# Weight sums started in the first half, stored blocks reloaded later, one activation sum moved by a product, held weights loaded into other buffers

## The chip, the cores and the metric

The kernel runs on one core of a Trainium2 chip. The metric is the device time of one execution in microseconds (us), the median over the runs shown. Five engines work side by side and meet only at semaphores: PE (matrix products), DVE (elementwise work on vectors), ACT (activation functions and copies), POOL (a second elementwise engine) and SP, which here issues every DMA transfer, one after the other in a fixed order.

## The reference

One decoder layer over 1024 tokens of 1024 features, in float32:

```
h   = rms_norm(x)
mix = [rwkv7_head_group(h), conformer_conv_group(h)] @ w_out
x   = x + rms_norm(mix)
h   = rms_norm(x)
hid = causal_conv3(h @ ffn_up)            # 1024 -> 2 * 2816 columns, 3 taps along the tokens
f   = (gelu(hid[:, :2816]) * hid[:, 2816:]) @ ffn_down
x   = x + rms_norm(f)
```

The change is only in the last part: the up projection, the gate and the down projection of the feed-forward block.

## The kernel before

**Precision.** Each float32 operand of a matmul is split into a rounded part and the rest, `hi` and `lo`. A product is then three matmuls: hi by hi, hi by lo and lo by hi. `split` (L154) lets ACT copy the rounded part and another engine subtract it to get the rest: POOL for streamed weights, DVE for activations. `weight` (L159) takes a buffer of tag `wr` (three of them, 128x512 floats each), lets SP load 256 KB into it, and splits it to `wh` and `wl` (two buffers each). With `held=True` the two parts go to buffers of the pool `h` instead, which stay full until the last product, and DVE rather than POOL makes the rest.

**Up projection.** Tokens are taken in two halves of 512. The 2816 gated columns are 22 blocks of 128. `ffn_pair` (L861 on) makes one gated block of one half: two projections of 1024 by 128 by 512, each with two weight tiles, then bias, three-tap convolution, gelu and product. Of the first half, blocks 0 to 11 are computed inside the mixer stage, wherever PE has room. Blocks 0 to 7 stay in on-chip rows; blocks 8 to 11 are stored to memory (`early`) and loaded back by `ffn_up` (L887 on; the load is L901). `ffn_up` then makes the ten blocks left of the first half, and after it the 22 of the second half. After some of these pairs it advances a generator `side` by one step, in a context that puts the step's DVE and POOL instructions behind the pair's last gate product and last weight split on these engines. DMA issues, ACT and PE instructions of the step are not bound by it.

The generator of the first half is the norm of the second half's rows (`norm_ffn`, L820 on): four steps, one for each 128 rows, and then `channels`, which transposes the last rows and writes their hi and lo parts. `islice` stops after four, so `channels` stands in the program behind all ten pairs. The generator of the second half is `weight_sums` (L915 on): 11 steps, each of which loads four 256 KB blocks of `ffn_down` into buffers of tag `tp` (eight of them), makes four sums on POOL (L918) and stores them to memory (L924 to L930). It is advanced after every second pair.

**Down projection.** `ffn_down` (L948 on) computes the product of the 1024 by 2816 gated matrix with the 2816 by 1024 weights as a 2 by 2 block scheme with seven block products in place of eight, called P1 to P7 here in the order of the code. Each has 11 steps `j`; a step splits one activation block (`a`, eight pairs of buffers ahead), splits one weight tile, and issues 12 matmuls. P1, P3, P5 and P7 sum into the four banks X, and P2, P4 and P6 into the four banks Y. P1, P3 and P7 take blocks of `ffn_down`, the others take the stored sums. Between them DVE makes the activation sums: in P4 `A22 += A21`, in P5 `A11 = A22 - A11` and then `A12 = A12 - A11`. P6 reads A11 and P7 reads A12. Seven weight tiles of P7 are held: `hold` loads and splits them during P5 (four) and P6 (three), so that P7 can end bank by bank. `second` after P6 and `last` after P7 finish the rows: norm, residual row from memory (`x1d`, L940), store to `out` (L946).

**Buffers of tag `f2`.** Six of 128x512 floats, used one after another by the up projection's accumulators, the norm's pieces, P2's activation differences, the scratch of P3's norm, and the residual rows of `ffn_out`.

**Order.** A planner orders each engine's instructions before the run, by priority (the place in the program, moved ahead for blocks marked high priority) and by its own estimate of times. Whatever has its inputs and its buffer may be placed ahead of work that stands earlier in the program. Buffers of one tag are given out in that order. On the chip each engine, and SP's queue of transfers, keeps the planned order: an instruction that waits holds all those behind it.

Of the kernel before, what the change touches and what calls it, by code (L numbers as in the profile page):

```python
# [4 lines left out]

# [8 lines left out]
F32 = mybir.dt.float32  # L14
# [38 lines left out]
EARLY, KEPT, EVERY = 12, 8, 2  # L53
# [42 lines left out]
class Trunk:  # L96
# [62 lines left out]
    def weight(self, src, shape, home=None, held=False):  # L159

        with self.tc.high_priority():
            raw = self.wp.tile(shape, F32, tag="wr", bufs=3, name=self.nm("wr"))
            self.nc.sync.dma_start(raw, src)
            if held:
                hi, lo = (self.hp.tile(shape, F32R, tag="h", name=self.nm("w")) for _ in range(2))
            elif home:
                hi, lo = (home[0].tile(shape, F32R, tag=t, bufs=BUFS[t], name=self.nm("wm")) for t in home[1:])
            else:
                hi, lo = (self.wp.tile(shape, F32R, tag=t, bufs=2, name=self.nm(t)) for t in ("wh", "wl"))
            self.low = self.split(hi, lo, raw, not held)[1]  # L170
        return hi, lo
# [715 lines left out]
    def ffn_up(self, h, hs, side, every, early=()):  # L887

        temp = lambda: self.f2p.tile([P, HALF], F32, tag="f2", name=self.nm("acc"))
        acts = []  # L890
        for i in range(FT):
            if i < min(KEPT, len(early)):
                acts.append(early[i])
                continue
            if h == 1 and i < 2 * KT:
                act = self.hp.tile([P, HALF], F32, tag="h", name=self.nm("act"))
            else:
                act = self.ap.tile([P, HALF], F32, tag="act", name=self.nm("act"))
            acts.append(act)
            if i < len(early):  # L900
                self.nc.sync.dma_start(act, early[i])  # L901
                continue
            self.ffn_pair(h, hs, i, temp, act)
            if (i - len(early)) % every == every - 1:
                with self.tc.issue_after(self.gated.ins), self.tc.issue_after(self.low.ins):
                    next(side, None)
        return acts
# [40 lines left out]
    def ffn_down(self, acts):  # L948
        nc = self.nc
        first = self.tc.high_priority  # L950
        A11, A12, A21, A22 = acts[0][:HT], acts[0][HT:], acts[1][:HT], acts[1][HT:]
        B = lambda r, c: lambda j: self.a["ffn_down"][c, r * HT + j]
        T = lambda n: lambda j: self.sums[n - 1, j]
        X = [self.bank() for _ in range(4)]
        Y = [self.bank(("pb", "pn")[t // 2]) for t in range(4)]
# [3 lines left out]
        def tt(out, a, b, op=ALU.add):  # L959
            nc.vector.tensor_tensor(out, a, b, op)  # L960
            return out
# [4 lines left out]
        def product(banks, src, wt, start, after, then=lambda j: None, held=(), soon=True):  # L966
            ops, n = [], HT - len(held)
            for j in range(HT):
                with first():
                    hi, lo = self.pair("a", self.h1p)  # L970
                    self.split(hi, lo, src(j))
                    then(j)
                wh, wl = self.weight(wt(j), [P, 512]) if j < n else held[j - n]
                op = (hi, wh), (hi, wl), (lo, wh)
                if j >= n:
                    ops.append(op)
                else:
                    for t in range(4):
                        mms(banks[t], t, op, start and j == 0, j == HT - 1)

            ins = []
            for t in range(4):
                for i, op in enumerate(ops):
                    ins += mms(banks[t], t, op, False, i == len(held) - 1)
                with first() if soon else ExitStack():
                    after(t)
            self.chain(ins)
# [27 lines left out]
        def after5(j):  # L1015
            hold(j, 3)
            tt(A11[j], A22[j], A11[j], ALU.subtract)
            tt(A12[j], A12[j], A11[j], ALU.subtract)

        product(Y, lambda j: A22[j], T(4), False, lambda t: tt(c21[t], s1[t], Y[t]), after4)  # L1020
# [12 lines left out]
            norm(0, t, 1, s1[t], s1[t], X[t])  # L1033
            self.ffn_out(t, (c11[t], s1[t]))

        product(Y, lambda j: A11[j], T(2), True, second, hold, soon=False)
        product(X, lambda j: A12[j], B(1, 1), False, last, held=late)


    def run(self):  # L1040
        self.setup()
        sts = [{}, {}]
        with ExitStack() as ctx:
            self.setup_mixer(ctx)
            h0, early = self.mixer(sts)
        with ExitStack() as ctx:
            self.setup_ffn(ctx)
            h1 = []
            norm = self.norm_ffn(1, lambda: self.row("nrow", 4),
                                 lambda: self.f2p.tile([P, HALF], F32, tag="f2", name=self.nm("m")), h1, 3,  # L1050
                                 pool=self.h1p)
            acts = [self.ffn_up(0, h0, islice(norm, 4), 1, early)]
            list(norm)
            side = self.weight_sums()
            acts.append(self.ffn_up(1, h1, side, EVERY))
            list(side)
            self.ffn_down(acts)

    def mixer(self, sts):
# [227 lines left out]
```

## Time and profile before

| | us |
|---|---|
| median of 3 runs | 1325.73 (1325.17 to 1326.6) |
| the profiled execution | 1324.09 |
| its span | 1322.3 |
| PE busy in the span | 1266.0 (96%) |
| DVE, ACT, POOL busy | 879.0, 680.5, 614.1 |
| up projection of the first half's last ten blocks starts, by the first of its matmuls | 727.4 |
| first matmul of the tile `w` (the held weights of P7) | 1292.5 |

PE is the engine to watch: it is busy nearly all of the time, and wherever it is idle the end moves. A view by stages gives, for each stretch of the span, the busy time of each engine (with the number of instructions), the granted PE clock as a share of full speed, the busy share of the DMA engines and the rate in GB/s. A row of a timeline gives start, duration, engine, line, operation, output from inputs and, in brackets, how long the engine had been idle and what released it. A row of waits gives who waited for whom: total us, times, longest.

### The profile page before, as it was taken

What the parts mean: (1) busy time and instruction counts of PE and PEld (TensorE: products, weight loads), DVE (VectorE), ACT (ScalarE), POOL (GpSimd) and SP (SyncE); (2) the same over time, 40 slices, a digit from 0 to 9 for tenths busy, and PEclk for the clock granted to TensorE, in tenths of its full rate; (3) what the DMA queues carried; (4) which work ended last, traced back from release to release, by engine and by line L of the source; (5) the groups of instructions that cost most, each with busy time, mean ns of one, the idle gap of its engine ahead of it and who ended that gap; (6) DMA issues with size and microseconds to landing.
All of it is one profiled execution on the core that took longest, in us unless ns stands there. A gap on an engine that the chain in (4) does not pass through costs nothing.

```text
span 1322.3 us, 22962 instructions
## 1 busy us (share of the span) xinstructions
PE 1266.0 (96%) x8580; PEld 1018.6 (77%) x8580; DVE 879.0 (66%) x1450; ACT 680.5 (51%) x1354; POOL 614.1 (46%) x522
## 2 busy tenths in 40 slices
PE   6999989999899989999999999999999999999996
PEld 5767767787679867787799778888888887877785
DVE  5376998997699979895521454355555559279447
ACT  6563654657655764656643464433433344543451
POOL 4343423344333422444463444476766666454541
PEclk9999989999999988999999999999999999999999
DMA  6222211121123441222354843356565643333436
GB/s 216 80 78 62 65 49 49 50 73 49 56 69 105 128 170 34 73 65 79 91 154 137 296 158 91 95 175 205 170 209 170 206 134 115 96 113 115 133 95 206
DMA packets 85647, 155.79 MB, mean 118 GB/s; under 512 B 9280, under 2 KB 15808, under 8 KB 85536
## 3 DMA queue, kind: packets, MB, share of 16 engines
q1 hardware_dynamic: 85536, 154.33, 38.0%
q8 instruction: 67, 1.10, 0.4%
q14 instruction: 44, 0.36, 0.1%
HBM read 129.13 MB, written 25.17 MB: 117 GB/s over the span
## 4 chain that ended last, share of the span: by engine, by line
PE 70%; DVE 14%; ACT 4%; issue 4%; DMA 4%; POOL 3%; SPq 0%; POOLq 0%; ACTq 0%; DVEq 0%
PE pb L130 57%; PE pe L130 4%; DVE pc L399 4%; PE xs L130 3%; POOL wl L157 2%; PE pn L130 2%; DVE dw L576 1%; DMA wr<-sums 1%; ACT wh L157 1%; DVE nrow L960 1%; PE pe L145 1%; DMA b<-ffn_down 1%; DVE kk L469 1%; DVE h L263 1%; DVE pt L468 1%
## 5 line engine op out<-in xcount | busy, mean ns | idle before, releaser
L157 POOL TENSOR_TENSOR wl<-wr,wh 128x512 fp32r<-128x512 f32 x350 | 468.0, 1338 | 536.7 <-ACT wh L157 509.0
L130 PE MATMUL pb<-f,wh 128*128 128x512 f32 x1408 | 444.2, 397 | 2.8 <-ACT pb L771 1.8
L157 ACT CAST wh<-wr 128x512 fp32r<-128x512 f32 x350 | 215.0, 615 | 325.0 <-PE pb L130 169.7
L130 PEld LDWEIGHTS pb<-f,wh 128*128 128x128 f32 x1408 | 264.4, 189 | 62.4 <-ACT pb L771 2.0
L130 PE MATMUL pb<-f,wl 128*128 128x512 f32 x704 | 281.0, 399 | 3.0 <-POOL wl L157 2.8
L130 PE MATMUL pb<-h,wh 128*128 128x512 f32 (+3 forms) x720 | 228.9, 398 | 2.0 <-ACT wh L157 1.4
L877 DVE SCALAR_TENSOR_TENSOR acc<-pb,params,acc 128x511 f32<-128x511 f32 (+1 forms) x128 | 95.5, 746 | 174.1 <-ACT acc L872 116.6
L399 DVE SCALAR_TENSOR_TENSOR pc<-c,params,pc 128x512 f32<-128x512 f32 x232 | 174.2, 751 | 4.6 <-ACT pc L396 0.5
L130 PEld LDWEIGHTS pb<-f,wl 128*128 128x128 f32 x704 | 133.0, 189 | 38.1 <-POOL wl L157 7.2
L130 PEld LDWEIGHTS pb<-h,wh 128*128 128x128 f32 (+2 forms) x720 | 131.5, 188 | 34.1 <-ACT wh L157 3.3
L130 PE MATMUL pb<-h,wl 128*128 128x512 f32 (+3 forms) x360 | 146.2, 406 | 2.8 <-POOL wl L157 2.6
L130 PE MATMUL pb<-wh,a 128*128 128x512 f32 x428 | 140.2, 395 | 1.5 <-ACT wh L157 1.5
L130 PEld LDWEIGHTS pb<-wh,a 128*128 128x128 f32 x428 | 80.3, 188 | 21.1 <-ACT wh L157 1.9
L130 PE MATMUL pb<-wl,a 128*128 128x512 f32 x214 | 85.3, 398 | 1.7 <-POOL wl L157 1.5
L130 PEld LDWEIGHTS pb<-h,wl 128*128 128x128 f32 (+2 forms) x360 | 67.5, 188 | 21.9 <-POOL wl L157 5.4
L157 DVE TENSOR_TENSOR a<-act,a 128x512 fp32r<-128x512 f32 x50 | 41.5, 837 | 41.8 <-ACT a L157 41.8
L157 ACT CAST a<-act 128x512 fp32r<-128x512 f32 x50 | 31.1, 621 | 63.5 <-PE pn L130 40.1
L877 DVE SCALAR_TENSOR_TENSOR pt<-pb,params,pt 128x511 f32<-128x511 f32 (+1 forms) x48 | 35.8, 746 | 35.7 <-ACT ecarry L874 35.3
L918 POOL TENSOR_TENSOR b<-b,b 128x512 f32<-128x512 f32 x44 | 58.3, 1324 | 0.9
L130 PEld LDWEIGHTS pb<-wl,a 128*128 128x128 f32 x214 | 40.2, 188 | 13.3 <-POOL wl L157 3.8
L872 ACT ACTIVATE acc<-pb,params 128x512 f32<-128x512 f32 x64 | 49.5, 773 | 1.8 <-PE pb L130 1.8
L130 PE MATMUL pn<-wh,a 128*128 128x512 f32 x132 | 46.7, 394 | 0.0
(297 smaller groups left out, 1947.1 us busy)
## 6 DMA issues: line engine op xcount, KB each, us to landing
wr<-ffn_up SPq DMA_DIRECT2D x176, 256.0 KB, 2.7
wr<-w_in SPq DMA_DIRECT2D x80, 256.0 KB, 2.6
b<-ffn_down SPq DMA_DIRECT2D x44, 256.0 KB, 3.9
sums<-b SPq DMA_DIRECT2D x44, 256.0 KB, 2.9
wr<-sums SPq DMA_DIRECT2D x44, 256.0 KB, 2.7
wr<-ffn_down SPq DMA_DIRECT2D x33, 256.0 KB, 2.6
wr<-w_out SPq DMA_DIRECT2D x32, 256.0 KB, 2.7
mixd<-t SPq DMA_DIRECT2D x16, 256.0 KB, 3.7
```

Source lines behind the costliest of these rows:

```text
L130: return self.nc.tensor.matmul(out, lhsT, rhs, start=start, stop=stop, skip_group_check=skip)
L145: self.nc.tensor.transpose(out, in_, self.con("ident")[:n, :n])
L157: return self.nc.scalar.copy(hi, src), eng.tensor_tensor(lo, src, hi.bitcast(F32), ALU.subtract)
L263: self.mark_lo = nc.vector.scalar_tensor_tensor(lo[:, toks], pv, g, hi[:, toks].bitcast(F32), ALU.mult, ALU.subtract)
L399: nc.vector.scalar_tensor_tensor(out, c[:, j:j + HALF], w(j), acc, ALU.mult, ALU.add)
L468: nc.vector.tensor_tensor_scan(sg[:, l], self.con("scan"), sg[:, l], 0.0, ALU.mult, ALU.add)
L469: nc.vector.scalar_tensor_tensor(kk[:, l], k[:, l], self.par("k_k", 2 * pp + l), kk[:, l], ALU.mult, ALU.mult)
L576: nc.vector.tensor_tensor(dv[:, j + 1:, :j], dv[:, j + 1:, :j], tv, ALU.add)
L872: nc.scalar.activation(acc, ps, AF.Identity, scale=w(2), bias=self.par("fb", ch))
L877: nc.vector.scalar_tensor_tensor(acc[:, o:], ps[:, :HALF - o], w(j), acc[:, o:], ALU.mult, ALU.add)
L918: sub = lambda o, x, y, op=ALU.subtract: nc.gpsimd.tensor_tensor(o, x, y, op)
L960: nc.vector.tensor_tensor(out, a, b, op)
```

## The change

Four edits, all in the feed-forward part.

1. The first half's `side` is now one generator that first runs the whole norm, `channels` included, and from its fifth step on advances `weight_sums` at every second step. With ten pairs these are steps 5, 7 and 9, so three of the eleven sum steps fall into the first half. The second half goes on with the other eight, still one after every second pair.
2. The four stored blocks are loaded back by DMAs that stand in the program behind the first half's ten pairs. Their buffers are taken at the same place as before.
3. `A12 = A12 - A11` moves from P5's hook to P6's.
4. The raw copy of a held weight is loaded into a buffer of tag `f2` instead of `wr`.

```diff
     def weight(self, src, shape, home=None, held=False):
 
         with self.tc.high_priority():
-            raw = self.wp.tile(shape, F32, tag="wr", bufs=3, name=self.nm("wr"))
+            raw = (self.f2p.tile(shape, F32, tag="f2", name=self.nm("wr")) if held else
+                   self.wp.tile(shape, F32, tag="wr", bufs=3, name=self.nm("wr")))
             self.nc.sync.dma_start(raw, src)
...
             if i < len(early):
-                self.nc.sync.dma_start(act, early[i])
                 continue
...
         def after5(j):
             hold(j, 3)
             tt(A11[j], A22[j], A11[j], ALU.subtract)
+
+        def after6(j):
+            hold(j)
             tt(A12[j], A12[j], A11[j], ALU.subtract)
...
-        product(Y, lambda j: A11[j], T(2), True, second, hold, soon=False)
+        product(Y, lambda j: A11[j], T(2), True, second, after6, soon=False)
         product(X, lambda j: A12[j], B(1, 1), False, last, held=late)
...
-            acts = [self.ffn_up(0, h0, islice(norm, 4), 1, early)]
-            list(norm)
-            side = self.weight_sums()
-            acts.append(self.ffn_up(1, h1, side, EVERY))
-            list(side)
+            sums = self.weight_sums()
+
+            def side():
+                yield from norm
+                while True:
+                    next(sums, None)
+                    yield
+                    yield
+
+            acts = [self.ffn_up(0, h0, side(), 1, early)]
+            for act, e in zip(acts[0][KEPT:], early[KEPT:]):
+                self.nc.sync.dma_start(act, e)
+            acts.append(self.ffn_up(1, h1, sums, EVERY))
+            list(sums)
             self.ffn_down(acts)
```

More of the change, by code (lines that the diff above doesn't have):

```diff
@@ L2 @@
 from contextlib import ExitStack, contextmanager
-from itertools import islice
 from types import SimpleNamespace
```

## The prediction

> **What bounds the kernel.** First the page's head and its busy line, then the stages of the feed-forward part.
>
> ```profile
> span 1322.3 us, 22962 instructions
> ...
> PE 1266.0 (96%) x8580; PEld 1018.6 (77%) x8580; DVE 879.0 (66%) x1450; ACT 680.5 (51%) x1354; POOL 614.1 (46%) x522
> ```
>
> ```profile
> 720.00:740.00 20.00, 18.20 (x102) 15.83 (x102) 3.35 (x5) 5.84 (x16) 3.86 (x3) 1.00 0.59 209
> 740.00:760.00 20.00, 18.41 (x77) 13.55 (x77) 12.66 (x18) 10.41 (x22) 9.66 (x9) 1.00 0.80 287
> 760.00:780.00 20.00, 19.48 (x88) 15.47 (x87) 10.84 (x16) 12.38 (x27) 9.99 (x10) 1.00 0.52 170
> 780.00:840.00 60.00, 60.00 (x278) 49.73 (x277) 25.73 (x43) 30.40 (x66) 28.05 (x23) 1.00 0.35 106
> 860.00:1080.00 220.00, 220.00 (x941) 176.72 (x940) 114.28 (x175) 86.60 (x137) 152.23 (x119) 1.00 0.58 184
> 1080.00:1100.00 20.00, 19.18 (x80) 14.54 (x80) 14.87 (x16) 12.05 (x21) 15.73 (x11) 1.00 0.41 132
> 1186.00:1217.00 31.00, 30.87 (x133) 24.53 (x132) 30.90 (x35) 14.04 (x28) 16.48 (x11) 1.00 0.45 144
> 1217.00:1250.00 33.00, 30.79 (x131) 24.22 (x130) 17.33 (x26) 14.79 (x26) 15.04 (x12) 1.00 0.40 121
> 1250.00:1281.00 31.00, 31.00 (x134) 24.92 (x134) 11.42 (x19) 13.60 (x24) 15.43 (x12) 1.00 0.41 118
> ```
>
> The first number behind each comma is PE's busy time. The last four stretches follow the products: P7 ends with PE at 1312.3 (row below), a product has 132 matmuls, and 220 us for 941 make 0.234 us each, so 31 us; P7 runs from 1281, P6 from 1250, P5 from 1217 with a gap in it, P4 from 1186. PE is the bound, at full clock (1.00). The change adds and removes no matmul, so it can only win PE's gaps or open new ones. They are few: 1.80, 1.59 and 0.52 us at the start, 0.82 at 1080, 0.13 at 1186 and 2.21 at 1217. From 780 to 840 and from 860 to 1080 there is none. PE's own waits from 640 on say what ended them:
>
> ```profile
> PE pb L130 <- POOL wl L157: 3.7, 9, 0.7
> PE pb L130 <- ACT pb L771: 1.8, 1, 1.8
> PE pb L130 <- ACT wh L157: 1.5, 1, 1.5
> ```
>
> The 1.8 behind L771 is the end of the mixer's output projection, which no edit touches. All else, 1.59 + 0.52 + 0.82 + 0.13 + 2.21 = 5.27 us, is PE waiting for a split weight tile. That is the whole prize: 0.4% of the run.
>
> **Held weights by other buffers, and the moved sum (edits 4 and 3).** The largest gap, in a timeline of SP, ACT, DVE and POOL where P4 ends and P5 begins, with the row of SP's waits that goes with it:
>
> ```profile
> 1211.52 0.33 SPq L163 DMA_DIRECT2D wr<-ffn_down  x1
> 1214.42 7.16 SPq L163 DMA_DIRECT2D wr<-sums  x3
> 1221.67 0.38 SPq L163 DMA_DIRECT2D wr<-ffn_down  x1
> ...
> 1214.16 0.62 ACT L157 CAST w<-wr 128x512 fp32r<-128x512 f32 x1 [1.67 <-DMA wr<-ffn_down]
> ...
> 1214.87 5.29 DVE L157 TENSOR_TENSOR a<-act,a 128x512 fp32r<-128x512 f32 x5
> 1220.08 0.68 DVE L157 TENSOR_TENSOR w<-wr,w 128x512 fp32r<-128x512 f32 x1
> ...
> 1224.28 1.82 POOL L157 TENSOR_TENSOR wl<-wr,wh 128x512 fp32r<-128x512 f32 x1 [4.67 <-ACT wh L157]
> ...
> SPq L163 <- DVE w L157: 11.2, 7, 6.0
> ```
>
> The first held tile is loaded at 1211.5 into one of three `wr` buffers. ACT has rounded it at 1214.8, but DVE makes its rest only at 1220.1, behind five activation splits. Until 1220.8 a third of the stream's buffers is gone and SP stands before its next transfer (the wait of 6.0). The weight tile behind it is split at 1224.3, and PE has lost 2.21 us. SP waited so for each of the seven held tiles, 11.2 us in all; by the windows only the long wait reached PE. So cover is about 6.0 - 2.2 = 3.8 us, an estimate: a shorter wait at SP is free.
>
> Edit 4 takes the held tiles out of `wr`, and the stream has its three buffers throughout. That removes this wait at its root, whatever DVE does: 2.2 us. The bounds are 1.5 (the ACT wait alone) and 2.2. The seven loads of 256 KB stay, in other places: six `f2` buffers are free when P3's scratch is done, and the place shows in what SP fills them with now:
>
> ```profile
> 1185.91 3.46 SPq L940 DMA_DIRECT2D x<-x1d  x6
> ```
>
> Six residual rows, needed only after P6. Held loads stand earlier in the program, so they should take these six places, at the same size and time. The 0.13 us lost from 1186 to 1217 therefore stays. The residual rows come one by one as held tiles are split; they are wanted by `second` after 1281, at least 30 us later, and cost nothing unless SP has to wait for their buffers (a rival below).
>
> Edit 3 moves eleven sums on DVE:
>
> ```profile
> L960 DVE TENSOR_TENSOR act<-act,row 128x512 f32<-128x512 f32 x8 | 8.5, 1069 | 0.0
> ...
> L960 DVE TENSOR_TENSOR act<-act,row x8: 677/688/1784, 1170.0 to 1204.4; 128x512 f32<-128x512 f32 x8
> ```
>
> Eleven at 1.07 us are 11.8 us. DVE is busy for 30.90 of 31 us in P4, where these sums of P5's hook are executed ahead of time, and for 11.42 of 31 in P6: moved there, P6 has 23.2 of 31 and PE still does not wait. P7's first splits need A12 and come up to eight blocks ahead, some 22 us, which is the cover. The planner may place part of them into the same early gaps as now, since A11 is ready; then DVE's load stays and only its order is better. Either way I count 0 on PE beyond edit 4: at most it shares the same 2.2 us.
>
> **Weight sums three steps earlier (edit 1).** The last step of `weight_sums` at present meets P1's first tiles on POOL:
>
> ```profile
> 1088.11 3.06 POOL L918 TENSOR_TENSOR b<-b,b 128x512 f32<-128x512 f32 x2
> 1091.14 1.81 POOL L157 TENSOR_TENSOR wl<-wr,wh 128x512 fp32r<-128x512 f32 x1
> 1092.91 1.75 POOL L918 TENSOR_TENSOR b<-b,b 128x512 f32<-128x512 f32 x1
> 1094.62 1.75 POOL L157 TENSOR_TENSOR wl<-wr,wh 128x512 fp32r<-128x512 f32 x1
> ```
>
> From 1088 to 1098 POOL runs without a pause, sums and splits in turn, and PE loses 0.82 us. With three steps done in the first half, the second half's eight end at its block 15 of 21, about six pairs before P1. POOL then has only splits here. Gain 0.8; bounds 0.5 (a fresh product still starts with an empty stream) and 0.8.
>
> What is added to the first half: 12 sums on POOL, 12 loads, 12 stores. A step's price is in the stage from 860 to 1080, which holds ten steps, and where PE is busy for 220.00 of 220 us with POOL at 152 (69%). The first half from 780 to 840 has POOL at 28.05 of 60; three steps of 4 by 1.32 us (58.3 / 44, L918's group on the page) add 15.9: 44 of 60, or 73%. So I take 0. The other end is the 0.82 of the step above, three times: 2.5 us lost. Nearest is the long stage, since it too splits one weight tile in 2.8 us (12 matmuls) and no activation.
>
> ```profile
> L918 POOL TENSOR_TENSOR b<-b,b 128x512 f32<-128x512 f32 x44 | 58.3, 1324 | 0.9
> ```
>
> `channels` gets its DVE part bound behind the fifth pair's gate product, about 727 + 5 x 11.2 = 783 us. Its amount is the same, DVE has 25.73 of 60 us there, and its result is first needed by the second half, 50 us later. I count 0.
>
> **Stored blocks reloaded later (edit 2).** SP's timeline at the start of the stage:
>
> ```profile
> 728.56 1.76 SPq L901 DMA_DIRECT2D act<-early  x4
> 730.37 2.03 SPq L843 DMA_DIRECT2D nrow<-x  x4
> 732.50 0.68 SPq L163 DMA_DIRECT2D wr<-ffn_up  x1
> 733.23 4.10 SPq L922 DMA_DIRECT2D b<-ffn_down  x5
> 738.33 0.33 SPq L163 DMA_DIRECT2D wr<-ffn_up  x1
> 739.57 1.69 SPq L922 DMA_DIRECT2D b<-ffn_down  x3
> 741.66 0.33 SPq L163 DMA_DIRECT2D wr<-ffn_up  x1
> ```
>
> Eight loads of weight sums, not needed before 860, have been placed ahead of the second and third weight tile, because their buffers are free. This crowd, and the reloads before it, cost PE 1.59 + 0.52 = 2.1 us from 740 to 780. The change does not thin out the eight; it moves 4 x 256 KB behind them. At the 287 GB/s of this stage that is 3.7 us of transfer. But what holds for the eight holds for the reloads: ready at once, they are likely to be placed in the next free slots, behind the eighth load, which SP has issued by 741.3, and still among these weight tiles. Bounds: 0 (same crowd in another order; 0.8 worse if four loads push a tile as half of the eight did) and 2.1. I take 0.5.
>
> **Sum.** 2.2 + 0.8 + 0.5 = 3.5 us less. The profiled execution took 1324.09 (span 1322.3), which would become 1320.6. The median of the runs shown stands 1.64 above it, at 1325.73: **1322.2 us**.
>
> The tail I leave as it is:
>
> ```profile
> 1292.53 19.76 PE L130 MATMUL pb<-w,a 128*128 128x512 f32 x84
> ...
> 1314.46 0.68 DVE L960 TENSOR_TENSOR nrow<-nrow,pb 128x512 f32<-128x512 f32 x1
> ```
>
> PE ends at 1312.3 and DVE takes up the last bank 2.2 us later, because residual rows arrive late through `f2`. The held tiles have left `f2` by then. Another order there may give or take 1 us.
>
> **Rivals.**
>
> *The wait moves to f2 (R1).* A residual row can be loaded only when DVE has split the held tile in its buffer, and SP keeps its order. If DVE lags behind the plan there, SP stands as it stood for 6.0 us, with weight tiles of the stream behind it. For it: DVE is full through P4, and at 1214.9 five splits stood ahead of the held one for 5.2 us. Against: the held tiles now arrive some 25 us earlier (1186 for 1211), and their splits no longer queue behind A12. One such wait gives the 2.2 back: 3.5 - 2.2 = 1.3 us faster, 1324.4. The row of L960 speaks for it: the same instruction took 0.677 or 1.784 us. [...]
>
> *The front clears (R2).* If the reloads leave the first 30 us, the 2.1 us go entirely: 2.2 + 0.8 + 2.1 = 5.1 faster, 1320.6. For it: they are the first four transfers now. Against: the eight loads were hoisted from much further. [...]
>
> *Slower (R3).* R1's mechanism at several places: up to eight rows and the seventh held tile wait for a split. Each wait of 6.0 us costs what is above the cover of 3.8, so 2.2. From three of them on, 6.6, the balance is +3.1: 1328.8. Against: all seven waits of today gave only one such.
>
> *Edit 2 changes nothing*, being hoisted again: 3.0 faster, 1322.7, within the forecast.
>
> **Chances.** The forecast 0.52, R1 0.24, R2 0.12, R3 0.12. The likeliest case alone reaches from 1320.6 to 1324.0. The range, 1319.6 to 1326.6, takes in R1 and R2, the tail's 1 us and R1's edge towards no gain, and leaves out most of R3. A difference under 0.2%, 2.65 us, can't be told from none. Faster: R2 and three quarters of the forecast, 0.52; the same: R1 and the rest, 0.35; slower 0.13.
>
> **What would show it.** P5's start without the gap, and no SP wait for DVE's `w` ahead of a `wr` load; if `x<-x1d` waits for `w` instead, R1. L918 from about 785, none in the last 60 us before P1, and POOL with pauses at 1088. `x<-x1d` not at 1186 but among the splits of `w`. The reloads (`act<-early`) must stand behind the third weight tile's load, 741.66 today, for edit 2 to have any worth, and PE's idle time from 740 to 780 shows it. The prediction is wrong if PE shows gaps from 780 to 840, or new waits for `wh` or `wl` in P4 to P6.

## The result, and the profile after

| | before | after |
|---|---|---|
| median | 1326.6 us (1325.17 to 1328.6, 5 runs) | 1340.2 us (1338.02 to 1341.92, 5 runs) |
| profiled execution, span | 1324.09, 1322.3 | 1338.02, 1336.2 |
| first half's matmuls start | 727.42 | 726.69 |
| P1 starts | 1091.76 | 1089.33 |
| held part (`w`) starts | 1292.53 | 1305.82 |

The change made the kernel slower: ratio 1.0101, 95% interval 1.0083 to 1.0118, so 13.6 us between the medians and 13.9 between the profiled executions. The prediction had 1322.2 with a range to 1326.6. (The ratios are estimates from all runs of both kernels, so they can differ a little from the quotient of the two medians.)

The table already says where. Up to P1 the changed kernel is 2.4 us ahead. From P1 to the held part it takes 216.49 us for 200.77, which is 15.7 lost; the tail adds 0.6. The page's head and busy line of the changed kernel:

```profile
span 1336.2 us, 22956 instructions
...
PE 1266.3 (95%) x8580; PEld 1019.7 (76%) x8580; DVE 860.7 (64%) x1450; ACT 679.6 (51%) x1354; POOL 618.8 (46%) x522
```

PE does the same work (1266.3 us for 1266.0). The view by stages, the first number behind the comma being PE's busy time and the third from the end the granted clock:

```profile
740.00:760.00 20.00, 18.85 (x81) 14.41 (x80) 10.50 (x19) 10.57 (x23) 10.41 (x10) 1.00 0.67 220
760.00:780.00 20.00, 20.00 (x93) 16.63 (x92) 11.82 (x20) 12.97 (x26) 10.43 (x10) 1.00 0.53 178
780.00:840.00 60.00, 60.00 (x277) 49.26 (x275) 28.41 (x42) 29.98 (x66) 43.22 (x35) 1.00 0.63 197
...
1080.00:1100.00 20.00, 16.50 (x65) 12.96 (x64) 14.19 (x24) 9.60 (x17) 12.46 (x6) 0.91 0.24 67
...
1200.00:1220.00 20.00, 9.47 (x29) 6.67 (x28) 14.44 (x25) 4.97 (x9) 10.93 (x3) 0.66 0.46 144
1220.00:1240.00 20.00, 20.00 (x87) 16.11 (x86) 9.43 (x12) 8.00 (x14) 8.51 (x8) 1.00 0.33 100
```

The start of the stage gained (740 to 780 has 1.15 us of idle for 2.11), and so did P5's start: 1220 to 1240 is full. The loss sits in two rows, 1080 to 1100 and 1200 to 1220, and both also show a lower clock. PE's own waits from 1080 on, first of the changed kernel, then of the kernel before:

```profile
PE pb L129 <- POOL wl L156: 11.3, 4, 7.5
PE pb L129 <- ACT wh L156: 3.4, 2, 3.0
```

```profile
PE pb L130 <- POOL wl L157: 1.5, 4, 0.7
PE pb L130 <- ACT wh L157: 1.5, 1, 1.5
```

So 14.7 us of waiting for 3.0. (Line numbers are one lower in the changed kernel; in the experiments they move by a few more.)

**The edits did what they say.** SP's timeline has the reloads behind the weight tiles, at 844 instead of 728, and the sums (second fence, the lines of POOL) run from 781 on and end 63 us ahead of P1:

```profile
844.40 1.85 SPq L1065 DMA_DIRECT2D act<-early  x4
```

```profile
L917 POOL TENSOR_TENSOR b<-b,b x44: 1284/1295/1307, 780.9 to 1024.6; 128x512 f32<-128x512 f32 x44
```

**P1: one POOL split takes 6.64 us.** Timelines of PE, POOL and DVE at P1's start:

```profile
1093.92 0.80 PE L129 MATMUL pb<-wl,a 128*128 128x512 f32 x1 [3.50 <-POOL wl L156]
...
1087.23 6.64 POOL L156 TENSOR_TENSOR wl<-wr,wh 128x512 fp32r<-128x512 f32 x1 [1.50 <-PE pb L129]
...
1087.24 2.49 DVE L156 TENSOR_TENSOR a<-row,a 128x512 fp32r<-128x512 f32 x4
1089.65 2.49 DVE L959 TENSOR_TENSOR s<-row,act 128x512 f32<-128x512 f32 x4
1092.06 0.69 DVE L156 TENSOR_TENSOR a<-row,a 128x512 fp32r<-128x512 f32 x1
1092.66 0.75 DVE L877 SCALAR_TENSOR_TENSOR acc<-pb,params,acc 128x511 f32<-128x511 f32 x1
```

POOL's split of one weight tile took 6.64 us. The groups of the same split by duration (min, median, max, in ns), after and before, show how far that is from all others:

```profile
L156 POOL TENSOR_TENSOR wl<-wr,wh x73: 1268/1292/8986, 1078.8 to 1301.5; 128x512 fp32r<-128x512 f32 x73
```

```profile
L157 POOL TENSOR_TENSOR wl<-wr,wh x73: 1290/1352/1848, 1081.2 to 1288.2; 128x512 fp32r<-128x512 f32 x73
```

Beside the long split stand nine DVE instructions with two on-chip inputs, one every 0.60 us without a pause. It ends 1.2 us (nearly a normal split of 1.29) after the start of the first DVE instruction that reads a product bank (`acc<-pb`, 1092.66). Its wait for a semaphore was over at 1087.23, where its row begins, and still it took 6.64 us. So in this trace the engines do not meet at semaphores alone, though the section on the chip says so. In the kernel before it was DVE that took longer at this place: POOL's sums and splits stood without a pause, none above 1.81 us, and the same four DVE splits took 5.79 us instead of 2.49:

```profile
1091.12 5.79 DVE L157 TENSOR_TENSOR a<-row,a 128x512 fp32r<-128x512 f32 x4
```

**P4: SP and ACT wait, then a POOL split takes 9.0 us.** SP's timeline, and its longest wait for DVE's splits from 1080 on:

```profile
1187.08 3.88 SPq L163 DMA_DIRECT2D wr<-ffn_down  x6
1191.06 0.38 SPq L163 DMA_DIRECT2D wr<-sums  x1
1200.29 0.33 SPq L163 DMA_DIRECT2D wr<-ffn_down  x1
1200.67 0.42 SPq L163 DMA_DIRECT2D wr<-sums  x1
```

```profile
SPq L163 <- DVE w L156: 8.5, 1, 8.5
```

Six held tiles fill the six `f2` buffers. The seventh load has to wait until DVE has split the first of them, and the next weight tile of the stream (`wr<-sums`) stands behind it in SP's queue, 9.6 us after the one before. That tile takes 3.0 us from issue to landing, so it is there at 1203.7:

```profile
wr<-sums SPq DMA_DIRECT2D x1, 256.0 KB, 3.0
```

By then ACT, which has to round it, stands still as well, in front of the rounded copy of the fifth held tile. ACT's timeline:

```profile
1203.91 0.62 ACT L156 CAST w<-wr 128x512 fp32r<-128x512 f32 x1 [5.98 <-DVE act L959]
```

That copy's data has landed some 9 us before. What ends the wait is a DVE sum at 1203.9, and the copy writes to the pool `h`, which activation blocks use as well; so it probably waited for a block that the sum was the last to read. The chain of work that ended last runs through this stop of ACT and not through SP's load (start, us, what):

```profile
1190.58 3.15 DMA wr<-ffn_down
...
1199.08 1.18 DVE w L156
...
1205.05 0.53 ACT wh L156
...
1205.64 9.00 POOL wl L156
```

A held tile has arrived at 1193.7, the first held rest comes at 1199.08, the late tile's rounded part at 1205.6 (PE has waited 3.04), and then its rest takes POOL 9.0 us, beside 13 DVE instructions in a row: 7.49 more for PE. The late load and ACT's stop end 0.2 us apart, and ACT's stop ends last; both go back to DVE, which comes late to its work. So the 3.04 us can't be put down to SP alone. All eight kernels here that load the held tiles into `f2` have both, ACT's stop with 5.7 to 7.4 us; where the held tiles use `wr`, ACT waits before them for loads alone, 2.1 us at most.

**The clock adds to it.** Stretches of the changed kernel, the granted clock third from the end:

```profile
1093.90:1097.00 3.10, 3.08 (x7) 2.49 (x8) 2.27 (x2) 0.00 (x0) 1.72 (x1) 0.50 0.46 116
1206.30:1207.20 0.90, 0.89 (x3) 0.17 (x1) 0.90 (x2) 0.00 (x0) 0.90 (x1) 0.50 0.84 287
1214.70:1219.90 5.20, 5.20 (x12) 4.12 (x13) 0.83 (x2) 1.66 (x3) 1.77 (x2) 0.50 0.72 202
1219.90:1225.00 5.10, 5.10 (x23) 4.09 (x22) 1.91 (x2) 1.55 (x3) 1.96 (x2) 1.00 0.31 103
```

After each of these idles (3.50, 3.04 and 7.49 us) the granted clock is 0.50; behind the last, PE makes 12 matmuls in 5.20 us and then, at 1.00, 23 in 5.10. At the 0.234 us of a matmul at full clock, the 7, 3 and 12 matmuls of the slow stretches would have taken 5.1 us; they took 9.2, an estimate of 4.1 us for the clock (1.5 behind P1's wait, 2.6 behind P4's). The whole stretch from P1 to the held part, after and before, bears that out:

```profile
1089.33:1305.82 216.49, 201.73 (x842) 160.24 (x840) 121.44 (x154) 95.07 (x179) 104.48 (x70) 0.96 0.34 98
```

```profile
1091.76:1292.53 200.77, 197.61 (x842) 157.23 (x840) 133.29 (x157) 95.96 (x181) 102.94 (x72) 1.00 0.37 109
```

PE is busy for 4.1 us more with the same matmuls and idle for 11.6 us more (14.76 for 3.16): together the 15.7. The clock was back at 1.00 after 3.1 us of work behind P1's wait and after 5.2 us behind P4's. The other kernels' timelines show it by the distance of the matmuls, 0.23 us at full clock. Behind P1's wait of 3.50 us they are 0.42 to 0.43 us apart with edits 1 to 3, and with edit 1 alone only from 1.9 us after its end on; behind P4's wait of 3.62 us they are so in the kernel with breaks and seven buffers. Behind the wait of 1.63 us in the kernel with two shifts they are not.

### The profile page after: what moved, and what is told of

Read it like the earlier page. It is cut to its first block, busy times and chain, and to the rows that moved or that the text cites. A ratio compares the mean times of both kernels' runs of the same rounds, so it can differ in the third digit from the quotient of the medians.

```text
span 1336.2 us, 22956 instructions
## 1 busy us (share of the span) xinstructions
PE 1266.3 (95%) x8580; PEld 1019.7 (76%) x8580; DVE 860.7 (64%) x1450; ACT 679.6 (51%) x1354; POOL 618.8 (46%) x522
## 5 line engine op out<-in xcount | busy, mean ns | idle before, releaser
L156 POOL TENSOR_TENSOR wl<-wr,wh 128x512 fp32r<-128x512 f32 x350 | 474.9, 1358 | 548.9 <-ACT wh L156 522.2
L129 PE MATMUL pb<-wl,a 128*128 128x512 f32 x214 | 86.7, 405 | 11.3 <-POOL wl L156 11.3
L156 DVE TENSOR_TENSOR a<-act,a 128x512 fp32r<-128x512 f32 x50 | 37.3, 746 | 66.1 <-ACT a L156 66.1
```

What stands on the lines that cost most here:

```text
L129: return self.nc.tensor.matmul(out, lhsT, rhs, start=start, stop=stop, skip_group_check=skip)
L156: return self.nc.scalar.copy(hi, src), eng.tensor_tensor(lo, src, hi.bitcast(F32), ALU.subtract)
```

## The experiments

Each run is read by its ratio to the kernel before and by the stretch from P1 to the held part in its profile. That stretch is the better measure of single edits, since the mixer before it, which none of the kernels changes, ends anywhere from 726.0 to 732.5 us in these profiles. The expectations name their theories by letters and say what each holds; the text below uses words.

| kernel | ratio, 95% interval | f stage to P1 | P1 to held part | PE waits in it (POOL, ACT) |
|---|---|---|---|---|
| before | 1 | 364.3 | 200.8 | 1.5, 1.5 |
| after | 1.0101, 1.0083 to 1.0118 | 362.6 | 216.5 | 11.3, 3.4 |
| only edit 4 | 1.0101, 1.0084 to 1.0117 | 364.6 | 211.7 | 8.4, 2.8 |
| edits 1 to 3 | 1.0017, 1.0003 to 1.0032 | 362.9 | 205.4 | 3.9, 1.4 |
| only edit 1 | 1.0034, 1.0019 to 1.0048 | 366.3 | 204.0 | 3.8, 1.4 |
| only edit 2 | 0.9995, 0.9982 to 1.0008 | 363.2 | 200.3 | 1.1, 1.4 |
| breaks | 1.0028, 1.0012 to 1.0044 | 363.7 | 205.1 | 1.8, 4.0 |
| breaks that read | 1.0087, 1.0066 to 1.0107 | 363.5 | 211.3 | 7.6, 3.5 |
| one shift | 1.0044, 1.0026 to 1.0063 | 363.2 | 211.1 | 8.3, 3.0 |
| two shifts | 1.0067, 1.0047 to 1.0086 | 363.3 | 209.5 | 3.3, 5.1 |
| seven buffers | 1.0109, 1.0084 to 1.0134 | 363.5 | 217.2 | 11.9, 3.5 |
| breaks, seven buffers | 1.0008, 0.9994 to 1.0022 | 363.7 | 204.7 | 1.6, 3.6 |
| edits 1 to 3, one shift | 0.9969, 0.9956 to 0.9983 | 363.6 | 198.4 | 0.5, 0.8 |
| held tiles in buffers of their own, one shift | 0.9966, 0.9953 to 0.998 | 363.1 | 198.7 | 0.5, 1.0 |

### Which edit costs it: edit 4 alone, and all but edit 4

```diff
 the kernel before, with edit 4 alone
-            raw = self.wp.tile(shape, F32, tag="wr", bufs=3, name=self.nm("wr"))
+            raw = (self.f2p.tile(shape, F32, tag="f2", name=self.nm("wr")) if held else
+                   self.wp.tile(shape, F32, tag="wr", bufs=3, name=self.nm("wr")))
```

> The kernel before with edit 4 alone (held tiles through f2). Theory F: the seventh held load finds six full buffers, SP stands before it for 6 us or more with weight tiles behind it, PE loses 8 to 11 us around the end of P4 in place of the 2.2 at P5's start: 1334 to 1339. Theory S: SP's wait alone costs 3 us, as much as the ACT wait in the changed kernel; more only if the late weight split falls into an unbroken run of DVE sums, which with A12's sums at their old place is not sure: 1326 to 1338, and if it is above 1331 a POOL split of over 5 us stands at that place.

Measured: 1337.68 us. POOL's splits and SP's wait of this kernel:

```profile
L157 POOL TENSOR_TENSOR wl<-wr,wh x75: 1272/1294/8988, 1080.2 to 1303.7; 128x512 fp32r<-128x512 f32 x75
```

```profile
SPq L164 <- DVE w L157: 8.3, 1, 8.3
```

The same 8 us wait of SP and the same 9 us split, and P1 untouched; ACT's stop is there too, with 5.7 us. Edit 4 alone makes 10.9 of the 15.7 us.

```diff
 the changed kernel, edit 4 taken back
-            raw = (self.f2p.tile(shape, F32, tag="f2", name=self.nm("wr")) if held else
-                   self.wp.tile(shape, F32, tag="wr", bufs=3, name=self.nm("wr")))
+            raw = self.wp.tile(shape, F32, tag="wr", bufs=3, name=self.nm("wr"))
```

> The changed kernel without edit 4 (held tiles through wr again; edits 1, 2 and 3 stay). Theory F: the gap of 11 us in P4 is gone, and P5's start has 0 to 2.2 us: 1324 to 1329, with P1's gap of 3.5 us left. Theory S: the same, if no weight split comes late; P1's start keeps a POOL split of over 5 us, since its cause is edit 1. If the gap in P4 stays, edit 3's order of DVE is the cause and not the buffers.

Measured: 1328.42 us. PE's waits from 1080 on:

```profile
PE pb L130 <- POOL wl L157: 3.9, 3, 3.5
PE pb L130 <- ACT wh L157: 1.4, 1, 1.4
```

P1's wait of 3.5 stays (a split of 6.63 us there), P4's are gone and P5's old gap is back, with 1.6 us for 2.2 (1.4 of it in the second row). The stretch is 4.7 longer than before; 10.9 + 4.7 = 15.6, so the two losses are separate and add up.

### Edits 1 and 2 by themselves

```diff
 the kernel before, with edit 1 alone
-            acts = [self.ffn_up(0, h0, islice(norm, 4), 1, early)]
-            list(norm)
-            side = self.weight_sums()
-            acts.append(self.ffn_up(1, h1, side, EVERY))
+            sums = self.weight_sums()
+            def side():
+                yield from norm
+                while True:
+                    next(sums, None)
+                    yield
+                    yield
+            acts = [self.ffn_up(0, h0, side(), 1, early)]
+            acts.append(self.ffn_up(1, h1, sums, EVERY))
```

> The kernel before with edit 1 alone (three sum steps in the first half). Theory S: with POOL free of sums at P1's start, its second weight split comes while DVE runs nine splits and sums of P1 and P2 in a row, and waits for their end: a POOL split of 5 to 7 us near 1088, PE idle for 3.5 us there in place of 0.8, 3 us at half clock behind it; P5's start keeps its 2.2: 1328 to 1331. Rival: the gap at P1 belongs to another edit (an order that the planner found for all four together), and this kernel gains the 0.8 us: 1325 to 1327.

Measured: 1328.73 us; P1 has a split of 6.63 us and a wait of 3.5, as above. So P1's loss comes with edit 1. DVE's instructions stand in the same order there in this kernel and in the one before. What differs is POOL: in the kernel before it was busy with sums from 1088 on and started its splits at other moments. In the first half PE has 58.84 of 60 us from 780 to 840, where the kernel before and the whole change have 60.00. The 1.16 us lost are PE waiting for a DVE instruction of `channels` (L263), not for a weight tile; the kernel with edits 1 to 3 has no such wait.

```diff
 the kernel before, with edit 2 alone
             if i < len(early):
-                self.nc.sync.dma_start(act, early[i])
                 continue
...
             acts = [self.ffn_up(0, h0, islice(norm, 4), 1, early)]
+            for act, e in zip(acts[0][KEPT:], early[KEPT:]):
+                self.nc.sync.dma_start(act, e)
             list(norm)
```

> The kernel before with the later reloads alone. If the prediction's term for edit 2 is right: the second half's front is 0.5 to 1 us shorter, nothing else moves, P1 and P4 to P6 are as in the kernel before; 1324 to 1326, ratio 0.999 to 1.000. If the earlier start of P1 by itself brings POOL into the lock-out (the moment, not the missing weight sums): a POOL split of 6 us or more in P1 and 1327 to 1329.

Measured: 1324.12 us beside 1325.33; the interval contains 1. In its view by stages:

```profile
740.00:760.00 20.00, 19.25 (x84) 15.14 (x83) 10.53 (x16) 10.50 (x24) 10.11 (x9) 1.00 0.62 214
760.00:780.00 20.00, 20.00 (x93) 16.62 (x92) 11.74 (x19) 13.26 (x29) 10.88 (x10) 1.00 0.57 190
```

Idle time from 740 to 780 is 0.75 us for 2.11, 1.4 less, which the time of this kernel cannot show. Most of that varies from profile to profile: edit 1 alone, with the reloads at their old place, has 1.22, and edits 1 to 3 have 1.55. What goes with the reloads is one pause of 0.5 us, 49 us into the stage: the three kernels that load them early have it, the eleven others don't. P1 has no long split, so the earlier start is not what brings it.

Edit 3 has no run of its own, but the traces tell of it. From P1 on DVE and ACT execute the same instructions in the same order with edit 1 alone as in the kernel before and with edits 1 to 3, and with edit 4 alone as in the whole change. So the eleven sums have the same places in whichever hook they stand.

### Is it DVE's run that makes POOL's splits long?

In the changed kernel, a VectorE instruction that reads nothing (a memset of 128x64, 112 ns) was put behind each activation sum, activation split and held split of the down projection:

```diff
+    def breathe(self, behind):
+        self.after(self.nc.vector.memset(self.gap, 0.0), behind)
...
-            nc.vector.tensor_tensor(out, a, b, op)
+            self.breathe(nc.vector.tensor_tensor(out, a, b, op))
...
-                    self.split(hi, lo, src(j))
+                    self.breathe(self.split(hi, lo, src(j))[1])
```

> The changed kernel with one thing added: behind each DVE sum or split of the down projection, DVE writes a scratch tile of 128x64 zeros, which reads nothing from SBUF. Theory S (starvation): a weight split on POOL cannot start while DVE runs instructions with two SBUF inputs back to back; the splits of 6.64 us at 1087 and 8.99 us at 1205 waited for such a train to end, and PE lost 3.5 and 7.5 us and then ran at half clock for some 3 and 5 us. With breaks in the train the longest POOL split falls below 3 us, PE's gap at P1's start goes to under 1 us, the one behind 1205 to about 3 (SP's wait for the seventh held tile stays): 1326 to 1329 us. Theory F (buffers): PE's gap in P4 comes from SP standing 8.5 us before the seventh held load, whatever DVE does; it stays about 10 us, and the time stays above 1335.

Measured: 1328.18 us, although DVE has 168 instructions and 18.8 us more to do. POOL's splits, PE's waits and SP's:

```profile
L156 POOL TENSOR_TENSOR wl<-wr,wh x74: 1288/1294/1857, 1080.1 to 1294.2; 128x512 fp32r<-128x512 f32 x74
```

```profile
PE pb L129 <- ACT wh L156: 4.0, 2, 3.6
PE pb L129 <- POOL wl L156: 1.8, 5, 0.7
```

```profile
SPq L167 <- DVE w L156: 8.5, 1, 8.5
```

No split is above 1.86 us, and the waits of 3.5 and 7.5 are gone. SP's wait and ACT's stop (6.6 us) are untouched, and PE still loses 3.6 there. So most of the loss goes with POOL's long splits, and the rest comes of these two waits.

The control puts a `tensor_tensor` of the same 128x64 there, with two on-chip inputs:

```diff
-        self.after(self.nc.vector.memset(self.gap, 0.0), behind)
+        g, z = self.gap[:, 0:64], self.gap[:, 64:128]
+        self.after(self.nc.vector.tensor_tensor(g, z, z, ALU.add), behind)
```

> The control of the kernel gap: the same number of small instructions on DVE at the same places, but each is a sum of two SBUF inputs of 128x64, and not a write without input. [...] Theory P (phase): any instruction that moves the moments helps as well, and no split is above 3 us: 1326 to 1331, as gap.

Measured: 1339.03 us. P1's long split is gone here too, P4's is back:

```profile
1203.64 9.56 POOL L156 TENSOR_TENSOR wl<-wr,wh 128x512 fp32r<-128x512 f32 x2 [6.80 <-ACT wh L156]
```

(8.32 us of it are the first split.) At P4 an instruction more in the run that reads two on-chip inputs does not help (8.32 us), one that reads nothing does (at most 1.86). But P1 was cured by this one as well, so the moment matters too, and since the two kinds of instruction also shift the work differently (112 and some 225 ns each), this pair of kernels does not tell the kind from the moment.

### Does the moment matter?

One memset of 128x64 between the first two activation splits of P1, in the changed kernel, and nothing else:

```diff
+                    low = self.split(hi, lo, src(j))[1]
+                    if mark is not None and j < 2:
+                        if j:
+                            shift = nc.vector.memset(self.gap, 0.0)
+                            self.after(shift, mark[0])
+                            self.after(low, shift)
+                        mark.append(low)
```

> The changed kernel with a single DVE write of 128x64 zeros (about 0.11 us) between the first and the second activation split of P1; the order of all else on DVE is that of the changed kernel, so the run of splits and sums behind it is whole. It only moves that run 0.1 us against POOL. Theory T (train): POOL cannot get in while DVE's run lasts, whatever the moment; a POOL split of over 4 us stays near 1088 and PE's gap there stays at 3 us or more: 1338 to 1341. Theory P (phase): the lock-out needs POOL to arrive within some 15 ns before to 45 ns behind the start of a DVE instruction, as the long splits seen so far did; moved by 0.1 us, POOL waits for one DVE instruction at most, its longest split near 1088 is under 2 us and PE's gap there under 1 us, with the gap in P4 as before: 1333 to 1337.

Measured: 1334.44 us. A shift of 0.11 us removes P1's long split (no split there above 1.9 us, PE's pause gone; the three other kernels with this shift agree, while all four that have edit 1 and neither shift nor breaks show a split of 6.63 to 7.23 us at P1); P4's stays, 8.99 us at 1206.16. In P4 the long split starts some 40 ns after the start of a DVE instruction in the changed kernel (1205.64 against 1205.60), with one shift (1206.16 against 1206.12) and with seven buffers (1210.96 against 1210.92), so it repeats.

The second shift, for P4, is a memset of 128x256 among DVE's work ahead of the long run, which itself stays unbroken:

```diff
         def after5(j):
             hold(j, 3)
+            if j == HT - 3:
+                shift = nc.vector.memset(self.gap4, 0.0)
+                self.after(shift, self.sum4)
+                self.after(tt(A11[j], A22[j], A11[j], ALU.subtract), shift)
+                return
             tt(A11[j], A22[j], A11[j], ALU.subtract)
```

(`tt` stands for the instruction that it issues; `sum4` is `A22 += A21` of the same step.)

> The whole change with the 0.11 us memset in P1 and a second one, of 128x256, that reads nothing and stands among VectorE's work of P4 ahead of the long run, so that the run starts some 0.2 to 0.3 us later against POOL's split and is itself unbroken. Theory P (the moment decides): P4's POOL split falls from 9.0 to under 2 us, TensorE keeps the 3.0 us wait for the ScalarE head (SP's 8 us wait for a buffer is untouched) and loses the 7.6 us one; 1326 to 1330. Theory T (an unbroken run of two-input work keeps POOL out whatever the moment): the POOL split of 8 to 9 us and the wait of 7 us or more stay, 1333 to 1336.

Measured: 1333.22 us. POOL's and DVE's timelines in P4:

```profile
1207.01 1.39 POOL L156 TENSOR_TENSOR wl<-wr,wh 128x512 fp32r<-128x512 f32 x1 [5.93 <-ACT wh L156]
1208.73 1.35 POOL L156 TENSOR_TENSOR wl<-wr,wh 128x512 fp32r<-128x512 f32 x1 [0.33 <-ACT wh L156]
...
1216.09 4.09 POOL L156 TENSOR_TENSOR wl<-wr,wh 128x512 fp32r<-128x512 f32 x1 [6.01 <-ACT wh L156]
...
1207.18 1.76 DVE L1030 TENSOR_TENSOR act<-act,act 128x512 f32<-128x512 f32 x1
```

The theory of the moment and that of the unbroken run each got half. The split that took 9 us now takes 1.39, with the same work beside it, and it is DVE that takes longer (1.76 for 0.68, in two instructions). But the next split but one takes 4.09 us, and with the slow clock most of the time is lost again. So in these kernels the long splits stand beside unbroken runs, and memsets of 0.11 and 0.27 us changed which split was long. The exact condition stays open: long splits started 10 ns before (1087.23 against 1087.24, the changed kernel) and 40 and 120 ns after the start of a DVE instruction (P4 above; 1216.09 against 1215.97, two shifts), and others that started 20 ns before one (1093.30 against 1093.32, one shift) and 20 ns after one (1205.13 against 1205.11, breaks) took 1.86 and 1.79 us.

### Is it the sixth buffer, or any?

Seven `f2` buffers, so that no held load needs to wait; first in the changed kernel, then in the one with breaks:

```diff
-        self.f2p = pool("f2p", 6)
+        self.f2p = pool("f2p", 7)
```

> The changed kernel with seven f2 buffers in place of six, so that the seventh held load needs no wait. Theory F: SP's wait of 8.5 us before a held load is gone, PE's 3.0 us for the late weight go, and since that tile is no longer late, the split that was locked out for 7.5 us meets DVE at another moment: P4's gap under 1.5 us in all. P1's gap of 3.5 and its slow clock stay: 1326 to 1329. If the lock-out in P4 belongs to DVE's order alone, a POOL split of over 5 us is still found between 1186 and 1217 and the time stays above 1333.

Measured: 1342.29 us. SP's waits:

```profile
SPq L939 <- DVE w L156: 10.3, 5, 8.0
```

The expectation failed. All seven held loads go out at once, and now the first residual row (`x<-x1d`, L939) stands before the stream and waits 8.0 us for the same split. ACT's stop before the fifth held tile is as long as before, 6.0 us, and ends 0.2 us after the late weight tile has landed. PE's pauses of 3.0 and 7.6 are as before.

> The changed kernel with both repairs: the breaks of gap, and seven f2 buffers. All theories: no POOL split over 2.5 us, no SP wait over 4 us before a held load, PE's gaps from P1 to P7 under 1.5 us in sum against 3.2 of the kernel before, and 1.0 us less at the start of the stage: 1321 to 1325, at or below the kernel before by 1 to 3 us. If it is slower than the kernel before, the 168 added DVE instructions (18.8 us in gap) cost something in the tail.

Measured: 1327.55 us, level with the kernel before. It fails in the same way: `x<-x1d` waits up to 7.6 us, ACT 6.5, PE 3.6. A buffer more moves SP's wait from one user of `f2` to the next and leaves ACT's as it is. No run here removes one of the two alone, so which of them PE's 3 us hang on stays open.

### Taking both causes away

The held raw tiles get seven buffers of their own, so that neither they nor the residual rows wait for one another, and the shift of P1 is kept. Each held load is ordered behind the stream's load before it, since free buffers would otherwise let the planner place all seven at the start of the stage:

```diff
-            raw = (self.f2p.tile(shape, F32, tag="f2", name=self.nm("wr")) if held else
+            raw = (self.f2p.tile(shape, F32, tag="hr", bufs=7, name=self.nm("wr")) if held else
                    self.wp.tile(shape, F32, tag="wr", bufs=3, name=self.nm("wr")))
-            self.nc.sync.dma_start(raw, src)
+            load = self.nc.sync.dma_start(raw, src)
+            if held:
+                self.after(load, self.stream_load)
+            else:
+                self.stream_load = load
```

> The whole change, but the seven held raw tiles take seven buffers of their own, outside both rings (each held load is issued behind the weight load that the stream issued before it, so that it is not issued early), and one VectorE memset of 128x64 (0.11 us, it reads nothing) shifts P1's activation splits. Theory A (the loss starts where SP waits for a buffer of the f2 ring on behalf of a held load or of a residual row; the POOL split of 9 us and the slow clock follow from it): SP has no wait above 4 us for a VectorE split in P4 to P6, TensorE waits neither 3 us for a ScalarE head nor 7 us for a POOL rest, P5's gap of 2.2 us is gone, and with P1's gap shifted away too the time is 1321 to 1325, below the kernel before by 1 to 4 us. Theory T (P4's lock-out is VectorE's unbroken run of two-input work alone, whoever waits): a POOL split of 7 to 9 us and a wait of 5 us or more at P4 stay, 1330 to 1334. A third: the seven tiles of their own change what SP issues when, and the wait only moves to another ring: 1326 to 1330.

Measured: 1320.4 us (1318.38 to 1323.6) beside 1325.33, ratio 0.9966, faster than both kernels. PE's waits from 1080 on, and POOL's splits:

```profile
PE pb L129 <- ACT wh L156: 1.0, 1, 1.0
PE pb L129 <- POOL wl L156: 0.5, 1, 0.5
```

```profile
L156 POOL TENSOR_TENSOR wl<-wr,wh x73: 1287/1299/1860, 1079.4 to 1284.3; 128x512 fp32r<-128x512 f32 x73
```

P4's long split and the slow clock are gone, though no instruction was put among DVE's there. Two waits went together: SP has none for a held split, and ACT waits before the held tiles for their loads alone, since the first of these now goes out at 1205.5 and not at 1187.1. The later loads also change DVE's order in P4. P5's gap has shrunk to 1.5, not to nothing. ACT's timeline says why:

```profile
1218.75 0.62 ACT L156 CAST w<-wr 128x512 fp32r<-128x512 f32 x1 [3.95 <-DMA wr<-ffn_down]
```

ACT rounds the held tile in its planned place, waits for that tile's data, and the stream's next rounded part stands behind it.

The last run leaves edit 4 out altogether and keeps the shift of P1 (the diffs of both are above):

> Edits 1 to 3 with the held weights through the weight ring as in the kernel before, and the 0.11 us memset that shifts P1's activation splits. Theory P (P1's 6.6 us POOL split hangs on the moment at which POOL asks): no POOL split above 2 us in P1, TensorE's 3.5 us wait there falls to under 1, P5's gap (about 2) stays since edit 4 is left out; 1323 to 1326, some 3 us below the same kernel without the memset and level with or up to 2 us below the kernel before. Theory T (any such run keeps POOL out): the 6.6 us split stays and the time is 1327 to 1330.

Measured: 1322.24 us (1320.39 to 1324.18), ratio 0.9969. The intervals of the two overlap almost wholly, and PE waits 1.3 us here for 1.5 there. So edits 1 to 3 and one memset have all the gain; edit 4 adds nothing that can be measured even when it does no harm.

## Why the prediction was wrong

**What bounds the kernel** was right: PE, at full clock, and only its gaps count. What was missing is that a gap has a second price. In the changed kernel the waits of 3.50, 3.04 and 7.49 us were each followed by a granted clock of 0.50, which cost an estimated 4.1 us, and no term of the sum held that.

**Edit 4: the step that failed** is "That removes this wait at its root, whatever DVE does: 2.2 us", with its companion that the residual rows "cost nothing unless SP has to wait for their buffers". The wait was removed from `wr` and came back at `f2`, longer, at the seventh held load: 8.5 us for 6.0. The prediction saw this mechanism as R1 and R3 (0.24 and 0.12) and counted too little for it. R1 priced one such wait at 2.2, R3's three at 6.6; by R3's own cover of 3.8 one wait of 8.5 would cost 4.7. PE lost 3.04 there, but ACT's stop, which the prediction did not have, ended later than the load, so that number says nothing of the cover. What no rival had either is the next step: the late tile's split then started in the middle of DVE's run and took 9.0 us, 7.49 more for PE, and the clock some 2.6. The place cost about 13.1 where R1 had 2.2. The gap of 2.2 at P5 did go, but it was also a smaller prize than counted: the other kernels that keep the held tiles in `wr` have 1.1 to 1.6 there in their profiles (1.6 in edits 1 to 3).

The argument against R1, that held tiles arriving 25 us earlier would be split earlier, failed by the row 1199.08: four were there at 1193.7, and DVE, full through P4, came to the first 5.4 us later. The second ground of R1, the row of L960, has DVE's instruction at 0.677 or 1.784 us; here it was POOL's instruction that took longer, 6.64 and 9.0 us for 1.29.

**Edit 1** was to gain 0.8, bounds 0.5 and 0.8, because "POOL then has only splits here". POOL did have only splits, and one took 6.64 us: PE waited 3.50 at P1 for 0.82, and about 1.5 went to the clock. The bounds reached to one side only, though the change moved the moments at which POOL's splits start beside DVE's. With the shift of 0.11 us the predicted gain is there: in the last two kernels P1 starts without a wait. That three steps cost nothing in the first half was right (60.00 of 60, with POOL at 43.22 where 44 was forecast). `channels`, counted at 0 as well, cost nothing in the whole change and 1.16 us with edit 1 alone.

**Edit 2** was counted at 0.5, bounds 0 and 2.1. The reloads were not hoisted into the crowd again, as the text thought likely; they went to 844. The pause of 0.5 us that goes with them is as large as the term; the view by stages gives 1.0 in the whole change and 1.4 alone, but the rest of that varies between profiles, and no time can show it.

**Edit 3** at 0 was right, for one of the reasons given: the sums stand in the same early places.

**The sum.** The two repaired forms are 4.5 and 4.1 us below the kernel before by their ratios, near the 3.5 of 2.2 + 0.8 + 0.5. That is luck: the form without edit 4 has as much of it, so the largest term has no part that shows. The lower edge of the likeliest case, 1324.0, does not come out of its bounds either: 1.5 + 0.5 + 0 gives 1323.7. And the chances of the cases add to 0.51 faster, 0.37 the same and 0.12 slower, not quite to the three that are given.

## What to carry to other kernels

When prefetches move to a ring that other transfers use, ask who frees that ring, what stands behind the waiting transfer in the issuing queue, and what stands behind the prefetched tile on the engine that takes it up; here another buffer only handed the wait to the next user. Where a POOL instruction on the critical path reads on-chip memory beside a long run of DVE instructions with two on-chip inputs, look at its largest duration, not its median (here 8.99 us and 1.29), and treat any change of timing there as able to cost several us (here 0.11 us of it went with a wait of 3.50 us on PE). Price a long gap on PE with the clock after it: in the changed kernel waits of 14.0 us in sum had an estimated 4.1 us of slow clock behind them.

## What the runs showed of the hardware

POOL's 128x512 split took 1.29 to 1.35 us at the median from P1 on, and at most 1.86 in the kernels without a long one. The long ones took 6.63 to 8.99 us (4.09 in the kernel with two shifts); in the changed kernel nine and thirteen back-to-back DVE instructions of 0.68 us each stood beside them. With a shift of 0.11 us there was none at P1, and with DVE instructions that read nothing between the others there was none at either place. In the kernel with two shifts two DVE instructions took 1.76 us (for 0.68) beside splits of 1.39 and 1.35.

PE's granted clock was 0.50 behind the waits of 3.50, 3.04 and 7.49 us of the changed kernel, and 1.00 in the stretch from 1200 to 1240 with the single waits of 1.5 and 1.4 us of the kernel before and of edit 2 alone.
